# A chunked recurrence in which v is centred while it is transposed

## The chip, the cores and the metric

The kernel runs on one core of one Trainium2 chip. The metric is the time of one execution on the device, in microseconds, as the median of several runs. TensorE does matrix products, DVE (VectorE), ACT (ScalarE) and POOL (GpSimd) do elementwise work, SP (SyncE) issues most of the transfers. Each of them has a queue of its own that it works through in the program's order.

## The reference

One block of a hybrid model on 1024 tokens of width 1024: two normed and modulated inputs, a softmax attention with forget gates ("fox", 8 heads of 64) beside a recurrence ("rwkv7", 8 heads of 64), their gated sum, and a convolutional feed-forward layer. Cut to what matters here, the recurrence keeps a 64 x 64 state per head and ends in a normalisation over the 64 value channels of each head:

```python
def step(state, inp):
    r_t, w_t, k_t, v_t, a_t, b_t = inp
    sa = jnp.einsum('bhvk,bhk->bhv', state, a_t)
    state = state * w_t[:, :, None, :] + sa[..., None] * b_t[:, :, None, :] + v_t[..., None] * k_t[:, :, None, :]
    y_t = jnp.einsum('bhvk,bhk->bhv', state, r_t)
    return state, y_t
...
mean = jnp.mean(y, axis=-1, keepdims=True)
var = jnp.mean(jnp.square(y - mean), axis=-1, keepdims=True)
y = ((y - mean) * lax.rsqrt(var + GN_EPS)).reshape(bsz, seq, RWKV_WIDTH) * ln_w + ln_b
bonus = (jnp.sum(r_h * k_h * r_k, axis=-1, keepdims=True) * v_h).reshape(bsz, seq, RWKV_WIDTH)
return ((y + bonus) * g).astype(p.dtype)
```

Every row of the state belongs to one value channel, and the rows never mix: state and y are linear in v, channel by channel. So a v whose mean over the 64 channels of a head is taken away gives a y whose mean is zero. The bonus needs v as it is.

## The kernel before, in words

The program has stages one after the other: norms and input products, the recurrence, the attention, the branch products, and the feed-forward layer. Large products are split in a high and a low part (three products in fp32r for one in fp32).

**Units.** The recurrence works on 8 units, one for each pair of heads p = 0..3 and half of the sequence hf = 0, 1; a unit has 8 chunks of 64 tokens. Names end in p_hf: X1_0 is the tile X of pair 1, first half. `pre` (L759 to L867) prepares a unit: decays, norms, the products p1 of keys and receptances inside each chunk, masked into E (L823), then v and the a-vectors transposed into `vt` and `at` (L843, L844) and copied to UV (ACT, L849) and QA (DVE, L850), and q (L861). `inverse` (L732 to L757), called the solve here, inverts the 32 x 32 triangles: 31 steps of two small DVE instructions each (L740, L744). Its matrix goes through DRAM on the way in (sm, then M, L831 and L835) and on the way out (se, then TT, L747 and L754). `main` (L869 to L974) takes TT up: DVE transposes a piece of it into X (two instructions, L881, one for each head), TensorE makes xi, zi, uw and mz, then the state is carried through the 8 chunks (sp, yp, L930 to L944).

**The tail of a unit.** y is copied from PSUM (L951). `head_sums` sums it over the 64 channels of each head: a cast to fp32r on ACT, the remainder on POOL, and two products with the block matrix blk_r (mu). DVE subtracts the mean (L959), ACT squares (L961), a second `head_sums` gives the variance (va), and DVE and ACT finish.

**What sets the order.** TensorE's order is written out while the program is built, by a planner (`Weave`) with a clock of estimated costs. Chains (`main_chain` for the units one behind the other, `pre_chain`, and a spawned solve for each unit) say with `yield n` that their next piece is due n nanoseconds later; until then the planner lays in pieces of other stages, the "big products" of 128x128 by 128x512 (ps_rkv, qk, v, gt). `main` waits for the planner's `ready` time of the unit's solve (L836, L879), but only if that lies ahead when its turn comes. DVE, ACT, POOL and SP are ordered by the scheduler of the language from the program's dependencies. PSUM has 4 banks for `gen` tiles and 2 for big products; DVE's L365, L391, L336 or L992 frees a bank of the latter.

Of the kernel before, what the change touches and what calls it, by code (L numbers as in the profile page):

```python
# [9 lines left out]
F32 = mybir.dt.float32  # L10
F32R = mybir.dt.float32r
AF = mybir.ActivationFunctionType
ALU = mybir.AluOpType
# [5 lines left out]
NH = 512  # L19
# [3 lines left out]
CH = 64  # L23
# [112 lines left out]
def hybrid_block(ctx: ExitStack, tc: tile.TileContext, a, out):  # L136
    nc = tc.nc
# [3 lines left out]
    def mm(o, lhsT, rhs, start, stop, more=False):  # L141

        weave.mm_cost(o, lhsT, rhs)
        weave.last = nc.tensor.matmul(o, lhsT, rhs, start=start, stop=stop, skip_group_check=more)  # L144
# [4 lines left out]
    def transpose(o, i, eye):  # L149
        weave.now += 0.84 * max(math.prod(i.shape[1:]), i.shape[0])  # L150
        nc.tensor.transpose(o, i, eye)  # L151

    def f32(ap):
        return ap.bitcast(F32)

    tt, stt, ts = nc.vector.tensor_tensor, nc.vector.scalar_tensor_tensor, nc.vector.tensor_scalar
# [19 lines left out]
    def C(name):  # L176
        o, k = CST[name]
        return cst[:, o : o + k] if o < NC1 else cst2[:, o - NC1 : o - NC1 + k]

    eye_r, tri_r = C("ident"), C("tri")  # L180
    ident, ones = f32(eye_r), f32(C("ones"))
# [160 lines left out]
    with ExitStack() as es:  # L342
# [7 lines left out]
        def gen(name):  # L350
            return pr.tile([128, NH], F32, tag="gen", name=name)
# [358 lines left out]
        rw = es.enter_context(tc.tile_pool(name="rw", bufs=1, reuse_waits="tile"))  # L710
# [9 lines left out]

        blk_r = rw.tile([128, 128], F32R, name="blk_r")
        nc.scalar.copy(blk_r, C("blk"))

        def head_sums(ps, x, hi, lo):

            nc.scalar.copy(hi, x)
            nc.gpsimd.tensor_tensor(lo, x, f32(hi), op=ALU.subtract)
            yield 3400
            mm(ps, blk_r, hi, start=True, stop=False)
            mm(ps, blk_r, lo, start=False, stop=True)  # L730
# [28 lines left out]
        def pre(k, p, hf):  # L759

            n = f"{p}_{hf}"
            cs = slice(hf * NH, hf * NH + NH)
            rr, kk, vv = rkv[p, hf]
# [52 lines left out]
            for c0 in range(0, NCU, 4):  # L816
                ps = [gen(f"p1_{n}{h}{c0}") for h in range(2)]
                for c in range(c0, c0 + 4):
                    for h in range(2):
                        mm(ps[h][:, (c - c0) * 128 : (c - c0) * 128 + 128], bk[HS[h], c, BKS[h], :], ar[HS[h], :, c, :],  # L820
                           start=True, stop=True)
# [18 lines left out]
            vt, at = gen(f"vt{n}"), gen(f"at{n}")  # L840
            for b in range(4):
                bs = slice(b * 128, b * 128 + 128)
                transpose(vt[:, bs], vv[:, bs], ident)  # L843
                transpose(at[:, bs], ar[:, 0, 2 * b : 2 * b + 2, :], ident)  # L844
            v4 = vt.rearrange("p (b h s) -> p b h s", h=2, s=CH)
            a4 = at.rearrange("p (b h s) -> p b h s", h=2, s=CH)
# [22 lines left out]
        def main(k, p, hf):  # L869
            o = units.pop((p, hf))  # L870
            n = f"{p}_{hf}"
# [38 lines left out]
            Zt = rw.tile([128, NCU, CH], F32, tag="Zt", name=f"Zt{n}", bufs=1)  # L910
            Mt = rw.tile([128, NCU, CH], F32, tag="Mt", name=f"Mt{n}", bufs=1)
# [11 lines left out]
            yp = py.tile([128, NCU, CH], F32, tag="yp", name=f"yp{n}")  # L923
# [23 lines left out]
                S0 = state[p] = S1  # L947
            passed.add((k, 1))

            y = rw.tile([128, NH], F32, tag="y", name=f"y{n}", bufs=1)  # L950
            nc.scalar.copy(y, yp.rearrange("p c s -> p (c s)"))  # L951

            def part(nm, i):
                return rw.tile([128, NH], F32R, tag=nm, name=f"{nm}{i}{n}", bufs=1)

            mu = gen(f"mu{n}")
            yield 700
            yield from head_sums(mu, y, part("Zt", "r"), part("Mt", "r"))
            stt(y, mu, -1.0 / CH, y, op0=ALU.mult, op1=ALU.add)  # L959
            ysq = rw.tile([128, NH], F32, tag="ysq", name=f"ysq{n}", bufs=1)  # L960
            nc.scalar.activation(ysq, y, AF.Square)  # L961
            yield 2700
            va = gen(f"va{n}")
            yield from head_sums(va, ysq, part("Zt", "s"), part("Mt", "s"))
            rs = rw.tile([128, NH], F32, tag="ysq", name=f"rs{n}", bufs=1)
# [37 lines left out]
        def pre_chain():  # L1003
            for k, (p, hf) in enumerate(order):
                while got[p, hf] < 3:
                    weave.step()
                yield from pre(k, p, hf)
                if p < 3:
                    weave.first.extend(rkv_items(p + 1, hf))
                yield 0  # L1010

        def main_chain():
            for k, (p, hf) in enumerate(order):
                while (p, hf) not in units:
                    yield 200
                yield from main(k, p, hf)
                yield 0
# [877 lines left out]
    for s, k in enumerate(ORDER):  # L1895
# [22 lines left out]
        for tp in range(4):  # L1918
            r = ssq[:, 16 + tp : 17 + tp]
# [86 lines left out]
```

## Time and profile before

| what | value |
|---|---|
| median of 3 runs | 1670.34 us (1670.2 to 1674.31) |
| profiled execution | 1675.3 us, span 1673.2 us |
| mean granted clock of TensorE | 0.986 |
| TensorE busy | 1622.3 us, 97% |
| DVE busy | 1227.8 us, 73% |
| ACT busy | 808.3 us, 48% |
| POOL busy | 147.8 us, 9% |

Of the span, the recurrence takes roughly 165 to 620 us. In rows of groups the columns are line, engine, operation, tiles written and read, shape and count, then busy time in us and mean of one in ns, then the engine's idle time before them and what ended it. In rows of the timeline they are the start in us, the length in us, engine, line, operation, tiles and count, and in brackets the idle time before and its releaser; a row may stand for several instructions in a row. In rows of waits they are the waiting engine and instruction, what ended the wait, the total in us, the number and the longest. In rows of windows they are the stretch, its length, then busy time and instructions of TensorE's products, its weight loads, DVE, ACT and POOL, the granted clock, the share of the DMA engines and GB/s. Products in fp32 (not fp32r) stand in the trace as two records each.

### The profile page before, as it was taken

How to read it: one execution, taken by the hardware profiler on the slowest of the kernel's cores; microseconds unless marked ns; L12 is line 12 of the kernel's file. 1: busy time of each engine (PE TensorE's matmuls, PEld its weight loads, DVE VectorE, ACT ScalarE, POOL GpSimd, SP SyncE). 2: the span in 40 equal slices, each digit the busy share in tenths (PEclk: the TensorE clock that was granted, in tenths of full speed). 3: DMA queues.
4: the chain of work that ended last, by engine and by line, in shares of the span. 5: the costliest groups of instructions: out<-in, count | busy, mean ns of one | idle time of the engine just before them, and what ended most of it. 6: DMA issues, size and time to landing. Idle time of an engine off the chain costs nothing.

```text
span 1673.2 us, 26056 instructions
## 1 busy us (share of the span) xinstructions
PE 1622.3 (97%) x9772; PEld 1333.2 (80%) x9772; DVE 1227.8 (73%) x2390; ACT 808.3 (48%) x1482; POOL 147.8 (9%) x175
## 2 busy tenths in 40 slices
PE   5899999999999998999999999999999999999998
PEld 4677877787977777888878888888888888888886
DVE  5786787888876635888778445897777777786677
ACT  5453343434455545767623244654444444455455
POOL 0010101111111012322022000000000000000000
PEclk8899999999999999999999999999999999999999
DMA  8497744433343236433197420143223323574463
GB/s 333 133 327 213 194 124 130 129 102 113 96 127 92 80 112 155 127 113 119 36 344 264 164 89 39 63 131 108 102 95 99 116 95 108 190 274 154 129 210 107
DMA packets 120974, 239.85 MB, mean 143 GB/s; under 512 B 39888, under 2 KB 48336, under 8 KB 120848
## 3 DMA queue, kind: packets, MB, share of 16 engines
q1 hardware_dynamic: 112896, 220.94, 40.8%
q0 software_dynamic: 7952, 17.25, 3.9%
q8 instruction: 77, 1.26, 0.3%
q14 instruction: 49, 0.40, 0.1%
HBM read 172.59 MB, written 65.54 MB: 142 GB/s over the span
## 4 chain that ended last, share of the span: by engine, by line
PE 82%; DVE 9%; DMA 4%; ACT 3%; issue 2%; SPq 1%; POOL 0%; DVEq 0%; ACTq 0%
PE X L144 13%; PE D L144 13%; PE Y L144 6%; PE gt L144 6%; PE ps_rkv L144 6%; PE wo L144 5%; PE br L144 5%; PE rk_ps L144 4%; PE W L144 3%; PE v L144 2%; PE lg L144 2%; PE ov L144 2%; PE tp L151 2%; PE qk L144 2%; PE low L144 1%
## 5 line engine op out<-in xcount | busy, mean ns | idle before, releaser
L144 PE MATMUL D<-op,op 128*128 128x512 f32 x924 | 209.8, 389 | 0.0
L144 PEld LDWEIGHTS D<-op,op 128*128 128x128 f32 x924 | 173.3, 188 | 36.3 <-DVE op L1269 0.3
L144 PE MATMUL X<-T_m,S 128*128 128x512 f32 x440 | 107.2, 390 | 0.1
L144 PEld LDWEIGHTS X<-T_m,S 128*128 128x128 f32 x440 | 82.4, 188 | 18.2 <-ACT T_m L1694 0.5
L1268 ACT CAST op<-g 128x512 fp32r<-128x512 f32 x77 | 47.8, 621 | 73.8 <-PE D L144 47.9
L1269 DVE TENSOR_TENSOR op<-g,op 128x512 fp32r<-128x512 f32 x77 | 53.0, 688 | 41.5 <-ACT op L1268 41.5
L1505 DVE SCALAR_TENSOR_TENSOR c<-ab,vec,c 128x512 f32<-128x512 f32 x88 | 65.8, 749 | 19.5 <-ACT c L1508 17.9
L1469 DVE TENSOR_TENSOR S<-ur,S 128x512 fp32r<-128x512 f32 x66 | 45.5, 691 | 35.9 <-ACT S L1465 35.7
L270 DVE TENSOR_TENSOR lo_in<-raw_in,hi_in 128x512 fp32r<-128x512 f32 x84 | 57.9, 727 | 14.0 <-PE gt L144 5.0
L1465 ACT CAST S<-ur 128x512 fp32r<-128x512 f32 x66 | 41.0, 622 | 55.8 <-DVE ur L1458 30.9
L1469 DVE TENSOR_TENSOR A<-ur,A 128x512 fp32r<-128x512 f32 x64 | 44.0, 687 | 30.9 <-ACT A L1465 30.7
L268 ACT CAST hi_in<-raw_in 128x1024 fp32r<-128x1024 f32 x42 | 43.9, 1048 | 44.4 <-PE ps_rkv L144 26.6
L740 DVE TENSOR_TENSOR t<-E,M 128x60 f32<-128x60 f32 (+24 forms) x248 | 56.0, 226 | 12.0 <-DMA M<-sm 5.7
L144 PE MATMUL Y<-T_h,A 128*128 128x512 f32 x264 | 63.5, 389 | 0.0
L144 PE MATMUL Y<-T_h,S 128*128 128x512 f32 x264 | 63.3, 389 | 0.0
L744 DVE TENSOR_TENSOR E<-E,t 128x60 f32<-128x60 f32 (+24 forms) x248 | 56.8, 229 | 5.8
L144 PE MATMUL X<-B_b,A 128*128 128x512 f32 x252 | 60.8, 390 | 0.0
L144 PE MATMUL W<-B_f,A 128*128 128x512 f32 x252 | 60.6, 389 | 0.0
L1090 ACT ACTIVATE P<-lg,nm 128x896 f32<-128x896 f32 (+3 forms) x64 | 47.4, 743 | 22.8 <-DVE nm L1086 22.6
L144 PEld LDWEIGHTS Y<-T_h,A 128*128 128x128 f32 x264 | 49.5, 188 | 10.4
L144 PEld LDWEIGHTS Y<-T_h,S 128*128 128x128 f32 x264 | 49.5, 188 | 10.3
L1465 ACT CAST A<-ur 128x512 fp32r<-128x512 f32 x64 | 39.8, 623 | 34.1 <-PE X L144 29.4
(473 smaller groups left out, 4151.9 us busy)
## 6 DMA issues: line engine op xcount, KB each, us to landing
raw_in<-in_w_in SPq DMA_DIRECT2D x50, 512.0 KB, 4.3
wm<-in_w_mod SPq DMA_DIRECT2D x48, 512.0 KB, 7.4
ur<-in_w_up SPq DMA_DIRECT2D x44, 512.0 KB, 4.3
g<-d_g SPq DMA_DIRECT2D x35, 512.0 KB, 3.9
d_g<-gs SPq DMA_DIRECT2D x44, 256.0 KB, 2.0
d_g<-c SPq DMA_DIRECT2D x33, 256.0 KB, 4.6
d_st<-qh SPq DMA_DIRECT2D x64, 128.0 KB, 2.4
d_gate<-gs SPq DMA_DIRECT2D x32, 256.0 KB, 2.7
```

Of the source, the lines that this page charges most:

```text
L144: weave.last = nc.tensor.matmul(o, lhsT, rhs, start=start, stop=stop, skip_group_check=more)
L151: nc.tensor.transpose(o, i, eye)
L268: nc.scalar.copy(hi, raw)
L270: nc.vector.tensor_tensor(lo[:, c : c + NH], raw[:, c : c + NH], f32(hi[:, c : c + NH]), op=ALU.subtract)
L740: i = tt(tv, E32[:, 0:J, s : s + 1].to_broadcast([128, J, W]), M32[:, s : s + 1, s + 1 : 32].to_broadcast([128, J, W]), op=ALU.mult)
L744: tt(E32[:, 0:J, s + 1 : 32], E32[:, 0:J, s + 1 : 32], tv, op=ALU.add)
L1090: nc.scalar.activation(e[:, 0:n], lg[:, 0:n], AF.Exp, bias=nm[:, 0:1], accum_out=nm[:, 1:2])
L1268: nc.scalar.copy(hi, src)
L1269: tt(lo, src, f32(hi), op=ALU.subtract)
L1465: nc.scalar.copy(hi, src)
L1469: tt(lo, src, f32(hi), op=ALU.subtract)
L1505: stt(c, ab[:, x + hf * NH : x + hf * NH + NH], V("conv_w", 22 * x + i), c, op0=ALU.mult, op1=ALU.add)
```

## The change

The block matrix blk, whose fp32r copy is kept in blk_r, is overwritten by cen = ident - blk / 64. In `pre` the transposes of v become products with cen as the moving operand: (v transposed) times cen is v transposed with the mean over the channels of each head taken away. y then has no mean. The first `head_sums`, its PSUM tile and the subtraction go; the square reads PSUM directly, ahead of the copy of y. The bonus still takes v as it was. The waits in the tail go from 700 + 3400 + 2700 + 3400 to 1300 + 3400.

```diff
         blk_r = rw.tile([128, 128], F32R, name="blk_r")
         nc.scalar.copy(blk_r, C("blk"))
+        cen = C("blk")
+        stt(cen, cen, -1.0 / CH, ident, op0=ALU.mult, op1=ALU.add)
...
             for b in range(4):
                 bs = slice(b * 128, b * 128 + 128)
-                transpose(vt[:, bs], vv[:, bs], ident)
+                mm(vt[:, bs], vv[:, bs], cen, start=True, stop=True)
                 transpose(at[:, bs], ar[:, 0, 2 * b : 2 * b + 2, :], ident)
...
+            yf = yp.rearrange("p c s -> p (c s)")
+            ysq = rw.tile([128, NH], F32, tag="ysq", name=f"ysq{n}", bufs=1)
+            nc.scalar.activation(ysq, yf, AF.Square)
             y = rw.tile([128, NH], F32, tag="y", name=f"y{n}", bufs=1)
-            nc.scalar.copy(y, yp.rearrange("p c s -> p (c s)"))
+            nc.scalar.copy(y, yf)
...
-            mu = gen(f"mu{n}")
-            yield 700
-            yield from head_sums(mu, y, part("Zt", "r"), part("Mt", "r"))
-            stt(y, mu, -1.0 / CH, y, op0=ALU.mult, op1=ALU.add)
-            ysq = rw.tile([128, NH], F32, tag="ysq", name=f"ysq{n}", bufs=1)
-            nc.scalar.activation(ysq, y, AF.Square)
-            yield 2700
+            yield 1300
             va = gen(f"va{n}")
             yield from head_sums(va, ysq, part("Zt", "s"), part("Mt", "s"))
```

How the order moves is shown at three places. A row has the line, the instruction, the tile written, the tiles read, and its shape; in the changed kernel the lines from L723 on are higher by two up to the tail, so L740 and L744 of the solve read L742 and L746, L850 reads L852 and L881 reads L883. Units are in the tiles' names.

On DVE, from the last instruction of the solve of unit 1_0 to the transposes of X1_0, before:

```order
L744 TENSOR_TENSOR E321_0_2651<-E321_0_2651,t321_0_2653 128x8
L823 TENSOR_TENSOR E1_1_3046<-p1_1_100_3049,cst2_120 128x4x128
L823 TENSOR_TENSOR E1_1_3046<-p1_1_110_3050,cst2_120 128x4x128
L270 TENSOR_TENSOR lo_in22_3074<-raw_in22_3071,hi_in22_3073 128x512 x2
L365 SCALAR_TENSOR_TENSOR k20_2753<-ps_rkv60_2997,omu_80,sh_rkv60_3066 128x512
L359 MEMSET sh_rkv100_3379 128x1
L959 SCALAR_TENSOR_TENSOR y0_1_3043<-mu0_1_3045,y0_1_3043 128x512
L823 TENSOR_TENSOR E1_1_3046<-p1_1_104_3100,cst2_120 128x4x128
L823 TENSOR_TENSOR E1_1_3046<-p1_1_114_3101,cst2_120 128x4x128
L270 TENSOR_TENSOR lo_v00_3134<-raw_v00_3131,hi_v00_3133 128x512 x2
L881 STREAM_TRANSPOSE X1_0_3200<-TT1_0_2524 32x256 x2
```

and the same place in the changed kernel:

```order
L852 COPY QA1_1_3049<-at1_1_3130 64x4x64 x2
L742 TENSOR_TENSOR t321_0_2741<-E321_0_2739,M321_0_2582 128x24
L852 COPY QA1_1_3049<-at1_1_3130 64x4x64 x2
L746 TENSOR_TENSOR E321_0_2739<-E321_0_2739,t321_0_2741 128x8x3
L742 TENSOR_TENSOR t321_0_2741<-E321_0_2739,M321_0_2582 128x16
L746 TENSOR_TENSOR E321_0_2739<-E321_0_2739,t321_0_2741 128x8x2
L742 TENSOR_TENSOR t321_0_2741<-E321_0_2739,M321_0_2582 128x8
L746 TENSOR_TENSOR E321_0_2739<-E321_0_2739,t321_0_2741 128x8
L883 STREAM_TRANSPOSE X1_0_3047<-TT1_0_2587 32x256 x2
L270 TENSOR_TENSOR lo_v00_3182<-raw_v00_3179,hi_v00_3181 128x512 x2
L365 SCALAR_TENSOR_TENSOR r20_2819<-ps_rkv20_3099,omu_80,sh_rkv20_3174 128x512
```

Before, nine rows of other work stood between the solve's end and X; now none does, and the copies of at1_1 to QA1_1, which came behind X, stand inside the solve.

On TensorE, at the transposes of unit 1_1 ahead of xi1_0, before:

```order
L151 MATMUL at1_1_3161<-cst_73,ar1_1_2902 128x128
L151 MATMUL vt1_1_3160<-cst_73,v11_2040 128x128
L151 MATMUL at1_1_3161<-cst_73,ar1_1_2902 128x128
L144 MATMUL ps_rkv100_3146<-u_hi_110,hi_in22_3073 128x512 x6
L144 MATMUL ps_rkv100_3146<-u_lo_111,hi_in22_3073 128x512 x4
L144 MATMUL va0_1_3121<-Zts0_1_3122,blk_r_1174 128x512
L144 MATMUL va0_1_3121<-Mts0_1_3123,blk_r_1174 128x512
```

(16 transposes tb1_1, the 16 small products q1_1 and then xi1_0 follow), and in the changed kernel:

```order
L144 MATMUL vt1_1_3129<-cst2_120,v11_2041 128x128
L151 MATMUL at1_1_3130<-cst_73,ar1_1_2916 128x128
L144 MATMUL vt1_1_3129<-cst2_120,v11_2041 128x128
L151 MATMUL at1_1_3130<-cst_73,ar1_1_2916 128x128
L144 MATMUL ps_rkv20_3099<-u_hi_110,lo_in14_3016 128x512 x3
L144 MATMUL xi1_0_3150<-X1_0_3047,E1_0_2434 32x32 x16
L144 MATMUL ps_rkv20_3099<-u_hi_110,lo_in14_3016 128x512 x5
L144 MATMUL ps_rkv100_3194<-u_hi_110,hi_in22_3093 128x512 x7
L144 MATMUL zi1_0_3202<-TT1_0_2587,X1_0_3047 32x32 x16
```

Ten big products, va, tb and q stood between the last at1_1 and xi1_0; now three big products do, and tb and q come after zi1_0.

On DVE, from the end of the solve of unit 2_1 to X2_1, before:

```order
L744 TENSOR_TENSOR E322_1_4690<-E322_1_4690,t322_1_4692 128x8
L802 TENSOR_TENSOR al3_0_4846<-al3_0_4846,k30_4068 128x512
L941 TENSOR_SCALAR S2_06_5099<-sp2_0_4905,pcd2_0_3556 128x64
L803 TENSOR_TENSOR bk3_0_5001<-al3_0_4846,en3_0_4994 128x8x64
L807 SCALAR_TENSOR_TENSOR ksq3_0_5013<-r30_4067,vec_72,al3_0_4846 128x512
L941 TENSOR_SCALAR S2_07_5111<-sp2_0_4905,pcd2_0_3556 128x64
L336 SCALAR_TENSOR_TENSOR gs0_0_5128<-gt0_0_5078,gs0_0_5128 128x512
L959 SCALAR_TENSOR_TENSOR y2_0_5115<-mu2_0_5117,y2_0_5115 128x512
L823 TENSOR_TENSOR E3_0_5155<-p1_3_000_5158,cst2_120 128x4x128
L823 TENSOR_TENSOR E3_0_5155<-p1_3_010_5159,cst2_120 128x4x128
L270 TENSOR_TENSOR lo_in15_5195<-raw_in15_5192,hi_in15_5194 128x512 x2
L881 STREAM_TRANSPOSE X2_1_5235<-TT2_1_4544 32x256 x2
```

and in the changed kernel, where the masks of p1_3_000 and p1_3_010 stand eleven solve steps ahead of the solve's end:

```order
L746 TENSOR_TENSOR E322_1_4772<-E322_1_4772,t322_1_4774 128x8
L825 TENSOR_TENSOR E3_0_5127<-p1_3_004_5153,cst2_120 128x4x128
L825 TENSOR_TENSOR E3_0_5127<-p1_3_014_5154,cst2_120 128x4x128
L270 TENSOR_TENSOR lo_in15_5181<-raw_in15_5178,hi_in15_5180 128x512 x2
L336 SCALAR_TENSOR_TENSOR gs0_1_5171<-gt0_1_5119,gs0_1_5171 128x512
L883 STREAM_TRANSPOSE X2_1_5005<-TT2_1_4640 32x256
L852 COPY QA3_0_5128<-at3_0_5208 64x4x64 x4
L883 STREAM_TRANSPOSE X2_1_5005<-TT2_1_4640 32x256
```

The end of the solve has moved closer to X2_1, and the copies of at3_0 lie between its halves. The number of gate products that the planner lays ahead of the attention is the same in both (18 halves of 24).

## The prediction

> **What bounds the kernel now.** I read the page's busy times, then the busy times of the stretch from 165 to 640 us in which the recurrence runs, then who TensorE waited for in it.
>
> ```profile
> PE 1622.3 (97%) x9772; PEld 1333.2 (80%) x9772; DVE 1227.8 (73%) x2390; ACT 808.3 (48%) x1482; POOL 147.8 (9%) x175
> ```
>
> ```profile
> 165.00:640.00 475.00, 465.11 (x4322) 375.01 (x4321) 342.19 (x959) 215.67 (x377) 66.51 (x83) 1.00 0.45 121
> ```
>
> ```profile
> PE rk_ps L144 <- ACT gm L1191: 4.6, 1, 4.6
> PE qk L144 <- DVE v L365: 2.2, 1, 2.2
> PE sp L144 <- DVE S L941: 1.5, 3, 0.9
> PE zi L144 <- ACT X L888: 0.6, 1, 0.6
> PE q L144 <- DVE QA L850: 0.4, 1, 0.4
> ```
>
> TensorE works 465 of these 475 us, at the full granted clock (1.00), since large products of other stages are laid between the steps of the recurrence. What it waits for adds up to 9.3 us, 4.6 of it at the start of the attention. So two things count here: TensorE's own work, and any wait that stops its one queue. Work taken off DVE, ACT or POOL is worth nothing by itself.
>
> **The change, part by part.** *The two products for the mean* go, 16 in all:
>
> ```profile
> 615.53 0.40 PE L144 MATMUL mu<-Ztr,blk_r 128*128 128x512 f32 x1
> 615.77 0.39 PE L144 MATMUL mu<-Mtr,blk_r 128*128 128x512 f32 x1
> 615.99 0.39 PE L144 MATMUL gt<-u_hi,hi_in 128*128 128x512 f32 x1
> ```
>
> From the first to the next stranger's start is 0.46 us, so 8 units give 8 x 0.46 = 3.7 us of TensorE back. *The four transposes of v* per unit become fp32 products with the matrix `cen`. The nearest rows are those transposes, and the fp32 products 128x128x128 of another stage (64 in the program, x128 in the trace, so each is two records):
>
> ```profile
> 176.41 0.27 PE L151 MATMUL vt<-cst,v 128*128 128x128 f32 x1
> 176.52 0.27 PE L151 MATMUL at<-cst,ar 128*128 128x128 f32 x1
> L144 PE MATMUL tr<-dg,h_sb 128*128 128x128 f32 x128 | 14.8, 275 | 0.0
> ```
>
> A transpose takes 0.11 us from start to start, a product 2 x 14.8 / 128 = 0.23 us. 32 of them cost 32 x 0.12 = +3.8 us. TensorE's own work thus stays where it was: -3.7 + 3.8 = +0.1 us (from -4, if they ran as the transposes do, to +3.8, if the removed pair had cost nothing; neither end is likely, with rows this near).
>
> The Trainium skill's page "TensorE: Matmul & The Clock Gate" (Terms) says that transpose mode is four times faster for FP32, and "Perfetto Trace Analysis" (Optimizing Tensor Performance) that a logical transpose should not be a standard matmul. By that the 32 products would cost 32 x 3 x 0.11 = +10.6 us and the sum below would end 6.8 us higher; the tr row of this trace says twice, not four times.
>
> *Off TensorE* go eight each of the DVE subtraction, the cast (like that of ysq) and POOL's low half:
>
> ```profile
> L959 DVE SCALAR_TENSOR_TENSOR y<-mu,y x8: 680/691/692, 269.2 to 616.8; 128x512 f32<-128x512 f32 x8
> L726 ACT CAST Zts<-ysq x8: 618/621/625, 270.6 to 618.2; 128x512 fp32r<-128x512 f32 x8
> L727 POOL TENSOR_TENSOR Mtr<-y,Ztr x8: 1284/1299/1320, 265.1 to 612.6; 128x512 fp32r<-128x512 f32 x8
> ```
>
> They take 0.69, 0.62 and 1.30 us. The ACT square now reads PSUM ahead of the copy of y, and one DVE instruction makes `cen` early on. None is on TensorE's path by the waits above, so I price them at nothing; if all of DVE's 8 x 0.69 = 5.5 us were on the path after all, that would be the gain of a rival below.
>
> *The yields* are the part that moves things. Ahead of the variance's products the planner now puts 1300 + 3400 in place of 700 + 3400 + 2700 + 3400, 5.5 us less per unit. The chains of the units run one behind the other, so the next unit's `xi` comes sooner, and it needs the solve (`inverse`), whose 62 small DVE instructions and two DRAM round trips stand where they stood. How tight this is, before:
>
> ```profile
> 568.49 0.18 DVE L744 TENSOR_TENSOR E<-E,t 128x8 f32<-128x8 f32 x1
> 568.73 2.52 SPq L747 DMA_DIRECT2D se<-E  x4
> 572.90 1.83 SPq L754 DMA_DIRECT2D TT<-se  x4
> 576.71 0.90 DVE L881 STREAM_TRANSPOSE X<-TT 32x256 f32<-32x256 f32 x2 [4.12 <-DMA TT<-se]
> 577.64 0.75 DVE L968 SCALAR_TENSOR_TENSOR y<-y,vec,rs 128x512 f32<-128x512 f32 x1
> 577.85 0.69 PE L144 MATMUL xi<-X,E 32*32 32x32 f32 x32
> ```
>
> That is the last unit. From the solve's last instruction (ended at 568.67) to the X transposes are 8.0 us of DMA there and back; DVE stands idle for 4.1 of them with y behind it, and xi starts 0.24 us after X. In the first unit the same trip took 219.91 to 226.13, and the second half 0.27 us more:
>
> ```profile
> 219.74 0.17 DVE L744 TENSOR_TENSOR E<-E,t 128x8 f32<-128x8 f32 x1
> 226.13 0.43 DVE L881 STREAM_TRANSPOSE X<-TT 32x256 f32<-32x256 f32 x1 [3.82 <-DMA TT<-se]
> ```
>
> I take 7.5 us, between 6.2 and 8.0. (In the changed order two loads of M for the next solve are issued on SP between se and TT of unit 1_0; SP waits there for se to land anyway, 571.25 to 572.90, so they cost nothing.) In unit 1_0 nothing waited before:
>
> ```profile
> 310.64 0.17 DVE L740 TENSOR_TENSOR t<-E,M 128x8 f32<-128x8 f32 x1
> 310.85 0.17 DVE L744 TENSOR_TENSOR E<-E,t 128x8 f32<-128x8 f32 x1
> 321.65 0.27 PE L151 MATMUL at<-cst,ar 128*128 128x128 f32 x1
> 321.90 0.89 DVE L881 STREAM_TRANSPOSE X<-TT 32x256 f32<-32x256 f32 x2
> 323.50 1.72 DVE L850 COPY QA<-at 64x256 f32<-64x256 f32 x4
> 326.44 0.69 PE L144 MATMUL xi<-X,E 32*32 32x32 f32 x32
> ```
>
> There the solve ended 10.9 us ahead of X, and the copies of `at` came behind X. In the changed order (the rows quoted with the change) the copies of `at1_1` stand between the last steps of the solve of 1_0, X stands right behind its last instruction, and on TensorE only three big products lie between the last `at1_1` transpose and `xi1_0`. DVE takes its queue in order, so the wait can be counted from that transpose on, whatever went on before:
> - four copies, 1.72 us, and six solve steps at 0.21 us (310.64 to 310.85), 1.3 us: 3.0
> - the trip, 7.5
> - X, 0.89, and 0.24 to xi: 1.1
>
> That is 11.6 us, less the three products that TensorE has meanwhile (0.23 each, by 615.77 to 615.99), 0.7: **TensorE stops for about 10.9 us at xi1_0** (9.6 with the trip at 6.2, 11.4 with 8.0; more where DVE runs late).
>
> In unit 2_1 (third place) X stood nine rows of DVE work behind the solve's end and now stands four behind it, and the `at3_0` copies lie between its two halves. From the end of the first `p1_3_0..` products on TensorE, DVE has 0.39 us to start, two masks, eleven solve steps, the trip, X, four copies, X:
>
> ```profile
> 318.37 1.29 DVE L823 TENSOR_TENSOR E<-p,cst 128x512 f32<-128x512 f32 x2 [0.39 <-PE p L144]
> 317.17 1.16 PE L144 MATMUL p<-ar,bk 64*128 64x128 f32 x16
> ```
>
> 0.39 + 1.29 + 11 x 0.21 + 7.5 + 0.43 + 1.72 + 0.43 + 0.24 = 14.3 us. TensorE has 28 big products (6.4), the second half of p (1.2 by the row) and the four vt and at (4 x 0.34 = 1.4), 9.0 us. Wait: 5.3 us.
>
> In unit 2_0 the DVE stretch from the `v` of the pair behind (L365, reading ps_rkv101) to the solve's end is 21 solve steps (4.4), two states (0.6), a scan (1.2), two splits (1.3) and four operations of 128x512 (2.9), 10.4 us; with ACT's shifted copy ahead (0.7), the trip, X with one y step between its halves (1.6) and 0.24 that is 20.4. TensorE has 62 big products (14.3), four steps of the state (4 x 0.38, from 309.43 to 309.81) and two pairs of sums (0.9), 16.7. Wait: 3.7 us, between nothing and 4.5.
>
> ```profile
> 309.43 0.33 PE L144 MATMUL sp<-S,Mt 64*64 64x64 f32 x4
> 309.81 1.65 PE L144 MATMUL ps_rkv<-u_hi,lo_in 128*128 128x512 f32 x6
> L362 ACT ACTIVATE sh_rkv<-ps_rkv,vec 128x512 f32<-128x512 f32 x24 | 16.6, 690 | 17.9 <-PE ps_rkv L144 16.5 <-issue 1.2
> L941 DVE TENSOR_SCALAR S<-sp,pcd 128x64 f32<-128x64 f32 x8 | 2.2, 279 | 2.2 <-PE sp L144 2.1
> L781 DVE TENSOR_TENSOR_SCAN cum<-cst,cum 128x512 f32<-128x512 f32 x1 | 1.2, 1217 | 0.0
> L803 DVE TENSOR_TENSOR bk<-al,en 128x512 f32<-128x512 f32 x1 | 0.7, 689 | 0.0
> ```
>
> The other five units keep their place: counted the same way, DVE's work and the trip end some 0.5 to 2.5 us ahead of xi, so DVE stands still there and TensorE does not. Behind X in unit 1_0 wait the split of w_v and the L365 that frees a bank; TensorE has 12 big products in hand there (2.8 us), which cover them.
>
> **The sum.** The products +0.1, unit 1_0 +10.9, 2_1 +5.3, 2_0 +3.7: +20.0 us. Against it, some of the 4.7 us of small waits before 620 us should fall away while the others catch up; I take 1.5. So +18.5 us, on the profiled execution's 1675.3 us about 1694. That execution is 5 us above the median of the runs (1670.34), so **1689 us** for the median. The stretch's own wait (4.6 us at rk_ps) stands behind it all and stays.
>
> **Rivals.**
> *No change, 1670 us.* The planner's order is tight on paper only: if the trip were short and DVE ahead, TensorE would wait for nothing, and the products cancel. For it: they do cancel, and the order has as many big products before the attention as it had. Against it: X cannot come before its own trip, whose shortest case here is 6.2 us, and 0.7 us of TensorE's work lies against it. Chance 0.10.
> *Faster, 1664 us.* DVE is busy 342 of 475 us, and the waits on it (2.2 + 1.5 + 0.4) with the 0.6 are 4.7 us. Were the freed 5.5 us of DVE to remove them all, and the products to cost as transposes (-3.7 in all), the time falls by up to 8 us, likely 6. It decides only if the moved X waits are absent. Against it: the 2.2 us stand at 228 us, in unit 0_0, where the order is as before. Chance 0.07.
>
> ```profile
> 228.11 1.21 PE L144 MATMUL qk<-u_hi,hi_in 128*128 128x512 f32 x4 [2.23 <-DVE v L365]
> ```
>
> *Only the one wait, 1680 us.* 2_0 and 2_1 are differences of large sums; if DVE is ahead there, 10.9 - 1.5 + 0.1 are left. Chance 0.20.
> *More, 1697 us.* The products at four times a transpose (+6.8), or DVE late into unit 1_0 and a bank not freed behind X (2.2 us in the first unit). Chance 0.10.
> The forecast, 1689, holds the remaining 0.53; its own range is 1683 to 1694.
>
> **The numbers.** A measurement of this kernel tells 0.3%, 5.0 us, from no change. Slower is the forecast, the one wait and more: 0.83; same 0.10; faster 0.07. The range from 1673 to 1697 leaves out the two cases that are not slower and a little above.
>
> **What would show it.** The waits of the changed kernel should have xi behind X (or X behind the DMA TT) as TensorE's largest, 9 to 12 us near 320 us, with DVE idle some 7 us just ahead of X there; a second of 3 to 7 near 475; `vt` as x64 records, 0.11 us each; TensorE's busy time in the page unchanged within 1 us. Wrong it is if xi follows the three ps_rkv products without a gap, or if the vt products take 0.4 us each.

## The result, and the profile after

| | before | after |
|---|---|---|
| median of 4 runs | 1672.32 us (1670.2 to 1674.43) | 1698.29 us (1696.5 to 1705.57) |
| profiled execution | 1675.3 us, span 1673.2 us | 1705.57 us, span 1703.8 us |
| mean granted clock of TensorE | 0.986 | 0.975 |

The changed kernel takes 1.0165 times as long, with a 95% interval of 1.0135 to 1.0196: 26 us by the medians, 30.3 us by the two profiled executions (that of the changed kernel is the slowest of its four). The forecast had the direction and the place, and was too small: 1689 us, in a range that ended at 1697.

Where the time lies is told first by the start of the attention, the first `lg` product. In the timeline of the kernel before it is

```profile
644.67 0.39 PE L144 MATMUL lg<-stA 128*128 128x512 f32 x1
```

and in that of the changed kernel

```profile
675.30 0.39 PE L144 MATMUL lg<-stA 128*128 128x512 f32 x1
```

30.6 us later. From there to the end of the span it is 1028.5 us in both. All that was lost, was lost ahead of that product. The windows from the start to the first `lg`, of the kernel before and of the changed one, split it (the second and third numbers are the length and TensorE's busy time):

```profile
0.00:644.67 644.67, 609.43 (x4916) 486.00 (x4916) 456.68 (x1130) 298.82 (x505) 79.94 (x105) 0.97 0.53 155
0.00:675.30 675.30, 619.80 (x4931) 496.42 (x4932) 450.98 (x1123) 292.14 (x497) 68.40 (x97) 0.95 0.50 149
```

TensorE is idle 55.5 instead of 35.2 us, 20.3 more, and busy 10.4 us longer. The waits of TensorE between 150 and 680 us of the changed kernel (what waits, what ended it, total in us, number, longest):

```profile
PE xi L144 <- DVE X L883: 18.4, 6, 10.8
PE rk_ps L144 <- ACT gm L1190: 4.8, 2, 4.6
PE qk L144 <- DVE v L365: 3.8, 1, 3.8
PE v L144 <- DVE lo_v L270: 2.3, 1, 2.3
```

Before, xi didn't wait at all. TensorE's timeline at the unit 1_0:

```profile
322.37 0.38 PE L144 MATMUL vt<-cst,v 128*128 128x128 f32 x2
322.59 0.27 PE L151 MATMUL at<-cst,ar 128*128 128x128 f32 x1
322.70 0.39 PE L144 MATMUL vt<-cst,v 128*128 128x128 f32 x2
...
323.62 0.95 PE L144 MATMUL ps_rkv<-u_hi,lo_in 128*128 128x512 f32 x3
335.38 0.28 PE L144 MATMUL xi<-X,E 32*32 32x32 f32 x2 [10.82 <-DVE X L883]
336.23 1.06 PE L144 MATMUL xi<-X,E 32*32 32x32 f32 x30 [0.56 <-DVE X L883]
337.21 2.50 PE L144 MATMUL ps_rkv<-u_hi,lo_in 128*128 128x512 f32 x5
```

DVE at the same place (the solve's last instruction, then X):

```profile
328.46 0.17 DVE L746 TENSOR_TENSOR E<-E,t 128x8 f32<-128x8 f32 x1
334.81 0.43 DVE L883 STREAM_TRANSPOSE X<-TT 32x256 f32<-32x256 f32 x1 [6.17 <-DMA TT<-se]
335.73 0.44 DVE L883 STREAM_TRANSPOSE X<-TT 32x256 f32<-32x256 f32 x1 [0.50 <-DMA TT<-se]
```

and SP with the trip through DRAM between them:

```profile
328.87 2.56 SPq L749 DMA_DIRECT2D se<-E  x4
...
332.85 1.80 SPq L756 DMA_DIRECT2D TT<-se  x4
```

This is the picture that was forecast: after `vt`, `at` and three big products TensorE has nothing it may do, and DVE stands idle for 6.2 us behind the trip. A `vt` product takes 0.22 us from its start to that of the next instruction, an `at` transpose 0.11.

What wasn't forecast stands in the last row: five big products from 337.21 to 339.51, 0.46 us each, where a big product took 0.23 us. The windows of the kernel before and of the changed one (the last three numbers are the granted clock, the DMA share and GB/s):

```profile
330.00:440.00 110.00, 109.15 (x1201) 93.88 (x1201) 89.35 (x266) 45.56 (x85) 16.57 (x22) 1.00 0.39 110
440.00:530.00 90.00, 89.89 (x845) 72.39 (x842) 70.92 (x203) 45.12 (x78) 12.59 (x16) 1.00 0.35 100
```

```profile
330.00:440.00 110.00, 100.23 (x1011) 84.00 (x1011) 76.35 (x229) 39.23 (x71) 11.31 (x20) 0.91 0.32 89
440.00:530.00 90.00, 84.33 (x937) 73.55 (x938) 62.74 (x181) 35.91 (x69) 8.98 (x13) 0.94 0.38 107
```

Before, the clock was granted whole. Now it is 0.91 and 0.94: it is halved for stretches behind the stops. By the trace's record of the granted clock there is one such stretch of 13.7 us from 329.2 us, one of 6.8 from 359.9, 3.4 from 441.9 and 6.8 from 506.7, and one of 6.8 from 230.2, where before there was none between 59.7 and 636.6 us. The stops that go with the last four, in TensorE's timeline:

```profile
230.90 1.22 PE L144 MATMUL qk<-u_hi,hi_in 128*128 128x512 f32 x2 [3.77 <-DVE v L365]
...
360.07 1.40 PE L144 MATMUL v<-lo_v,u_hi 128*128 128x256 f32 x4 [2.27 <-DVE lo_v L270]
...
440.23 0.22 PE L144 MATMUL xi<-X,E 32*32 32x32 f32 x2 [1.72 <-DVE X L883]
441.24 0.69 PE L144 MATMUL xi<-X,E 32*32 32x32 f32 x30 [0.79 <-DVE X L883]
...
506.39 0.22 PE L144 MATMUL xi<-X,E 32*32 32x32 f32 x2 [2.77 <-DVE X L883]
508.39 1.05 PE L144 MATMUL xi<-X,E 32*32 32x32 f32 x30 [1.78 <-DVE X L883]
```

Counted by their starts, 11, 12, 8 and 9 big products run at 0.43 instead of 0.23 us behind the stops at 230, 335, 440 and 506 us: 40 x 0.2 = 8.0 us. Behind that at 360 us stand none of 128x512, but 21 of 128x256, at 0.23 instead of 0.12 us (eight take 1.87 us from 362.02 on, three took 0.36 from 356.80): 2.3 us. That is 10.3 us of the 10.4.

### The profile page after: what moved, and what is told of

It is laid out like the page before. It is cut to its first block, busy times and chain, and to the rows that moved or that the text cites. A ratio compares the mean times of both kernels' runs of the same rounds, so it can differ in the third digit from the quotient of the medians.

```text
span 1703.8 us, 26049 instructions
## 1 busy us (share of the span) xinstructions
PE 1632.5 (96%) x9788; PEld 1343.6 (79%) x9788; DVE 1223.2 (72%) x2383; ACT 802.1 (47%) x1474; POOL 135.7 (8%) x167
## 4 chain that ended last, share of the span: by engine, by line
PE 82%; DVE 9%; DMA 4%; ACT 2%; issue 2%; SPq 1%; DVEq 0%; ACTq 0%
PE X L144 13%; PE D L144 12%; PE Y L144 6%; PE gt L144 6%; PE wo L144 5%; PE br L144 5%; PE ps_rkv L144 5%; PE rk_ps L144 4%; PE W L144 3%; PE qk L144 3%; PE v L144 3%; PE lg L144 2%; PE ov L144 2%; PE tp L151 2%; PE low L144 1%
## 5 line engine op out<-in xcount | busy, mean ns | idle before, releaser
L742 DVE TENSOR_TENSOR t<-E,M 128x60 f32<-128x60 f32 (+24 forms) x248 | 57.1, 230 | 10.9 <-DMA M<-sm 5.1
L746 DVE TENSOR_TENSOR E<-E,t 128x60 f32<-128x60 f32 (+24 forms) x248 | 55.6, 224 | 5.8
L144 PEld LDWEIGHTS Y<-T_h,A 128*128 128x128 f32 x264 | 49.5, 188 | 10.4
L144 PEld LDWEIGHTS Y<-T_h,S 128*128 128x128 f32 x264 | 49.6, 188 | 10.3
```

The costliest lines, as they stand in the source:

```text
L742: i = tt(tv, E32[:, 0:J, s : s + 1].to_broadcast([128, J, W]), M32[:, s : s + 1, s + 1 : 32].to_broadcast([128, J, W]), op=ALU.mult)
L746: tt(E32[:, 0:J, s + 1 : 32], E32[:, 0:J, s + 1 : 32], tv, op=ALU.add)
```

## The experiments

The theory after the result: the new order alone makes the loss; it consists of TensorE's stops at xi and of a halved clock behind each stop; the products with `cen` and the square that reads PSUM cost what was forecast. The rivals: the products cost more (four times a transpose), or the square and the copy now both reading PSUM hold something up; or one tight unit makes all of it. In the expectations the theory is Theory 1 and the dearer products or PSUM reads are Rival A; Theory 3 is that a stop costs its own length and no more.

**The old waits in the tail.** The changed kernel, with the time between the copy of y and the variance as it was, 700 + 3400 + 2700 = 6800:

```diff
-            yield 1300
+            yield 6800
```

> The changed kernel with the tail's wait of 1300 set to 6800, so that the order of the large products and the place of every X is as before (the distance from p1 to xi is within 1.5 us of the kernel before's in all units but 2_0, where it is longer). Theory 1 (the loss is the stops of TensorE at xi, and the halved clock that follows each): no wait at xi over 1 us, one halved stretch at most near 230 us, time 1668 to 1674. Rival A (the products with cen, or the square from PSUM, cost the time): no gain from the order, 1690 or more.

Measured: 1672.7 us (9 runs, 1666.43 to 1676.75), 0.9988 of before, interval 0.9971 to 1.0005. The waits in the same stretch:

```profile
PE qk L144 <- DVE v L365: 3.3, 1, 3.3
PE sp L144 <- DVE S L943: 2.4, 4, 0.8
PE rk_ps L144 <- ACT gm L1190: 1.4, 2, 1.2
```

No xi waits, the stop at rk_ps is 1.2 instead of 4.6 us, and that at qk stays (3.3 us, with a halved stretch of 3.4 us and 7 slow products behind it). One number was put back, all 32 products and the PSUM reads stayed, and the loss is gone. The order makes it; what the products and the PSUM reads add lies within the interval, some 3 us to either side.

**Transposes in place of the products**, in the order of the run before (the planner was told the products' cost). This kernel leaves the centring out:

```diff
-                mm(vt[:, bs], vv[:, bs], cen, start=True, stop=True)
+                transpose(vt[:, bs], vv[:, bs], ident)
+                weave.now += 160.32 - 107.52
```

> As the run with the old yields, but v is transposed again instead of multiplied with cen, so the mean of y is left out of the computation altogether; TensorE's order is row by row the same. This prices the 32 products by themselves. By the rows of the trace (0.23 against 0.11 us) it is 3.8 us below that run; if a product cost four transposes, 10.6 us below; if the products were hidden, equal.

Measured: 1667.83 us (6 runs, 1664.67 to 1671.48), 0.9956 of before (0.9941 to 0.997), 4.9 us below the run with the products. The forecast's row gave 3.8 us, the rule of four times 10.6. The intervals of the two ratios (each some 2.5 us to either side) don't tell 3.8 from 4.9; they leave 10.6 out. With the starts in the trace (0.22 and 0.11 us) a product costs about twice a transpose here.

**The solves called ready later.** If the planner knew that X comes later, it would put TensorE's work there, and the stops at xi would go:

```diff
-            ready = weave.now + (47500 if k == 0 else 38500)
+            ready = weave.now + (52000 if k == 0 else 47000)
```

> The changed kernel with the planner's ready time of a solve set to 47000 instead of 38500 ns after its load (52000 instead of 47500 for the first unit); the short tail stays. The distance from p1 to xi becomes 53 to 74 us. Theory 1: the waits at xi vanish, in the first unit too (3.8 us and its halved clock), so 1663 to 1671, at or below the kernel before. Rival A: no change from the changed kernel, 1690 or more. Theory 3 (a stop costs only its own length): also at about 1670, since the waits go.

Measured: 1695.95 us (4 runs, 1692.31 to 1699.57), 1.0119 of before (1.01 to 1.0139). A miss by some 25 us; the time is one that Rival A had named, but its cause is excluded by the first run. The waits, and the first `lg`:

```profile
PE sp L144 <- DVE S L943: 5.7, 4, 3.2
PE v L144 <- DVE vs L991: 3.5, 1, 3.5
PE lg L144 <- DMA stB<-d_st: 2.9, 1, 2.9
PE xi L144 <- DVE E L746: 2.6, 1, 2.6
```

```profile
665.27 0.39 PE L144 MATMUL lg<-stA 128*128 128x512 f32 x1
```

The xi waits went as meant, from 18.4 to 2.8 us. The chain of the units stayed long: the first `lg` is 20.6 us behind that of before, with 48 more big products (a gate, about 11 us) laid ahead of it. That work is missing in the attention: from the first `lg` to the end of the span (1697.8 us) are 1032.5 us, 4.0 more than in the changed kernel, although 11 us of products had been taken from there. The windows from the first `lg` to the end, of this run and of the changed kernel:

```profile
665.27:1697.80 1032.53, 1011.06 (x4810) 844.87 (x4808) 771.00 (x1258) 505.00 (x967) 66.35 (x70) 0.98 0.40 136
675.30:1703.80 1028.50, 1012.75 (x4858) 847.16 (x4856) 772.22 (x1260) 509.95 (x977) 67.28 (x71) 0.99 0.41 136
```

TensorE is idle 5.7 us longer there and busy only 1.7 us less, not 11. By the record of the clock it ran at half for 34.0 us of this stretch instead of 14.7, which is up to 9.6 us of slower products. So with fewer products to lay between, the stops moved on (to sp and v, and to lg and others in the attention), and there too they were paid with their length and with a halved clock.

**One unit called ready later**, that of the longest stop alone:

```diff
-            ready = weave.now + (47500 if k == 0 else 38500)
+            ready = weave.now + (47500 if k == 0 else 48500 if k == 2 else 38500)
```

> The changed kernel with the ready time of unit 1_0 alone later by 10000 ns: its distance from p1 to xi goes from 46.7 to 56.5 us, those of 2_0 and 3_0 fall by 2 to 3 us. Theory 1: the 11.4 us wait at xi1_0 falls to 2 us or less, with it the halved clock near 337 us (12 slow products, 2.4 us) and the 2.3 us wait of v_0 behind X with its own halved stretch: 12 to 16 us off, 1682 to 1687. Theory 3 (a stop costs only its own length): 9 to 10 us off, 1688 to 1690. Rival A: nothing off.

Measured: 1697.53 us (4 runs, 1696.56 to 1698.01), 1.0135 of before (1.012 to 1.0151): another miss, at the time of Rival A, whose cause the first run excludes. The wait row of xi, and the two units in the timeline:

```profile
PE xi L144 <- DVE X L883: 17.6, 6, 9.5
```

```profile
333.39 0.22 PE L144 MATMUL xi<-X,E 32*32 32x32 f32 x2 [2.04 <-DVE X L883]
...
433.65 0.28 PE L144 MATMUL xi<-X,E 32*32 32x32 f32 x2 [9.55 <-DVE X L883]
```

The stop of 10.8 us at xi1_0 shrank to 2.0; that of xi2_0 grew from 1.7 to 9.5. The sum of the xi waits is 17.6 instead of 18.4 us. So it isn't a single tight place: the stop goes to another unit when it is closed here. The starts of xi from unit to unit, in us, show the same:

| | from unit to unit | first to last |
|---|---|---|
| before | 49, 48, 47, 58, 47, 52, 47 | 349 |
| old waits in the tail | 49, 48, 47, 59, 47, 52, 47 | 350 |
| changed | 44, 60, 51, 54, 66, 50, 59 | 383 |
| one unit ready later | 43, 61, 43, 57, 69, 46, 59 | 378 |

Laid 5.5 us closer by the planner, the units come at 44 us once, and then at 60; the mean goes from 50 to 55 us.

**What a stop costs.** Onto the kernel with the old waits, one stop of chosen length was put in the fifth unit: 1, 4 or 18 copies of 128x256 on POOL, and a small product `dm` that needs the last of them. These copies and the product add work; their result isn't used.

```diff
+            if k == 4:
+                da = rw.tile([128, 256], F32, tag="X", name="da", bufs=1)
+                for _ in range(1):
+                    nc.gpsimd.tensor_copy(da, y[:, 0:256])
+                dm = gen("dm")
+                nc.tensor.matmul(dm[:, 0:256], ident, da, start=True, stop=True)
```

> The kernel with the old yields (no wait at xi), and one stop of TensorE put in by hand in unit 2_0, where it was never idle: behind the last yp it must wait for one POOL copy of a 128x256 piece of y, and then makes one small product that nobody reads. The stop is ACT's copy and the POOL copy, some 1.5 to 2 us. Theory 1 (a stop over about 2 us is followed by some us at half the granted clock, a shorter one mostly not): clock 1.0 throughout there, the stretch longer by the stop alone. Theory 3 (a stop costs its own length): the same.

> The same with four POOL copies: a stop of some 3 to 3.5 us. Theory 1: a stretch of 3.4 or 6.8 us at clock 0.5 begins at its end, with 7 to 14 big products at 0.43 instead of 0.23 us, 1.4 to 2.8 us on top of the stop. Theory 3: none of that.

> The same with eighteen POOL copies: a stop of some 9 us. Theory 1: the clock is at 0.5 during the stop, and for up to 6.8 us behind it; on top of the stop 1.4 to 2.8 us, no more than behind the middle one, since it is the time to come back that costs, not the length. Theory 3: none.

Measured, one execution each: 1673.32, 1684.61 and 1690.8 us, beside 1672.38 for the kernel before. In the timelines, the stop, the eight big products after it and the first `lg`; with one copy:

```profile
467.30 0.70 PE L962 MATMUL dm<-da,cst 128*128 128x256 f32 x2 [1.64 <-POOL da L960]
467.65 2.18 PE L144 MATMUL gt<-u_hi,lo_in 128*128 128x512 f32 x8
...
641.60 0.39 PE L144 MATMUL lg<-stA 128*128 128x512 f32 x1
```

with 4 copies:

```profile
476.50 1.22 PE L962 MATMUL dm<-da,cst 128*128 128x256 f32 x2 [7.36 <-POOL da L960]
477.16 3.98 PE L144 MATMUL gt<-u_hi,lo_in 128*128 128x512 f32 x8
...
653.58 0.39 PE L144 MATMUL lg<-stA 128*128 128x512 f32 x1
```

with 18 copies:

```profile
479.86 1.22 PE L962 MATMUL dm<-da,cst 128*128 128x256 f32 x2 [13.56 <-POOL da L960]
480.51 3.97 PE L144 MATMUL gt<-u_hi,lo_in 128*128 128x512 f32 x8
...
656.88 0.39 PE L144 MATMUL lg<-stA 128*128 128x512 f32 x1
```

The stops were meant to be 1.5 to 2, 3 to 3.5 and some 9 us. The two longer ones came out longer, since POOL took up other work between its first copy and the rest (4.4 us of it and of waiting, from 470.7 to 475.1 us, with four copies).

The eight products take 2.18 us behind the stop of 1.6 us, and 3.98 and 3.97 behind those of 7.4 and 13.6. From the beginning of the stop (start of `dm` less its idle time) to `lg` are 175.9, 184.4 and 190.6 us. Against the shortest that is 8.5 and 14.6 us more, for stops 5.7 and 11.9 us longer: the two longer stops cost 2.8 and 2.7 us on top of their length. In both, 11 big products and `dm` ran slow: from the start of `dm` to that of the next small product (p) it is 5.84 us, with one copy 3.14, 2.7 us less. So the addition is the same for a stop of 7 as for one of 14 us, and the stop of 1.6 us has none. The rest of the differences between the three times lies elsewhere, 3.5 us ahead of the stop with 4 copies and 1.9 us behind `lg` with 18.

**X laid behind the v of the first unit.** The stop at qk in the first unit stands because X is ahead of L365 in DVE's queue and waits for the trip there. With X due 300 ns ahead of `ready` instead of 1500, and xi 300 ns behind it (old waits in the tail):

```diff
-            yield max(0, o["ready"] - weave.now - 1500)
+            lead = 1500 if k else 300
+            yield max(0, o["ready"] - weave.now - lead)
...
-            yield 1500
+            yield lead
```

> The kernel with the old yields, and in unit 0_0 alone X is issued 300 instead of 1500 ns ahead of xi: on DVE X0_0 then stands behind the w_in split and the L365 that frees the bank, TensorE's order and the other seven units stay. Theory 1: the 3.3 us wait of qk at 227 us and its halved stretch (7 slow products, 1.4 us) go, xi0_0 waits at most 1 us: 3 to 5 us below the run with the old yields, 1667 to 1670, and 5 to 8 us below the kernel before. If DVE's head of queue was not the cause of that wait, it stays, and the time too.

Measured: 1671.39 us (12 runs, 1668.39 to 1674.06), 0.9988 of before (0.9978 to 0.9998), as without the edit. The timeline of TensorE tells why:

```profile
227.89 1.43 PE L144 MATMUL xi<-X,E 32*32 32x32 f32 x32 [2.32 <-DVE X L884]
229.25 3.78 PE L144 MATMUL qk<-u_hi,hi_in 128*128 128x512 f32 x8
```

qk no longer waits, but xi now does, 2.3 us. This stop is shorter than the one it replaced (3.3), and 12 slow products stand behind it instead of 7.

**And xi as far behind X as it was.** Same as the last, with the second wait left at 1500:

```diff
-            yield max(0, o["ready"] - weave.now - 1500)
+            yield max(0, o["ready"] - weave.now - (1500 if k else 300))
```

> The change with the old waits in the tail (6800 in place of 1300), and for the first unit alone the X transposes placed 300 ns instead of 1500 ns ahead of the due time of the solve, with xi 1500 ns behind them as it was. If a short stop is paid twice (its length, and a stretch of halved clock behind it), then taking away both the stop of 3.3 us at qk near 227 us, which X causes by standing ahead of L365 in DVE's queue, and the xi stop that takes its place when xi isn't moved too, gives the 3.3 us and the 1.4 us of slow products back: 1667 to 1669 us, with no stop over 1.5 us between 165 and 620 us and no halved clock there. If stops merely move on, as they did when one unit was made to wait, it stays at 1671 to 1673 with some other stop of 2 us or more in the first unit.

Measured: 1668.93 us (10 runs, 1665.81 to 1671.25), 0.9964 of before (0.9952 to 0.9976). The largest waits in the stretch, and the window that holds the first unit:

```profile
PE sp L144 <- DVE S L943: 2.2, 4, 0.8
PE sp L144 <- DVE sh_rkv L361: 1.4, 1, 1.4
PE rk_ps L144 <- ACT gm L1190: 1.4, 2, 1.2
```

```profile
220.00:330.00 110.00, 105.41 (x1020) 81.91 (x1020) 83.76 (x240) 43.48 (x77) 12.62 (x20) 1.00 0.49 130
```

No stop over 1.4 us, the clock whole from 54 to 705 us, and the time that was expected. This version computes all of the change and is faster than both kernels, by 5.6 us (before, in the same set of runs) and by some 29 (changed, by the medians of two sets).

## Why the prediction was right and wrong

**The products, +0.1 us: right.** `vt` takes 0.22 us and a transpose 0.11; with the old order the whole change stands at 0.9988 of before.

**The three stops: right in place and nearly in size.** Forecast 10.9, 5.3 and 3.7 us, measured 10.82 + 0.56 = 11.4 (1_0), 2.77 + 1.78 = 4.6 (2_1) and 1.72 + 0.79 = 2.5 (2_0); 18.4 for 19.9. The cause is as put there: X stands right behind the solve's end, and its trip through DRAM (6.2 us of idle DVE; X begins 6.2 us after the solve's last instruction ended) has 0.7 us of TensorE's work against it. That 1_0 came out so near was partly luck: the trip took 6.2 us instead of 7.5, but the solve ended 4.8 us behind the last `at` transpose instead of 3.0, since other steps still stood ahead on DVE, and X's second half waited another 0.5.

**The small waits, -1.5 us: right.** Those on S, X to zi, and QA went from 1.5 + 0.6 + 0.4 to 0.6 us, -1.9.

**"Twelve big products cover what is queued behind X": right at that place, and short-sighted.** Nothing waited in the ten us after xi1_0. But TensorE's v waited 2.3 us at 360 us for a split that DVE reached late, after solve steps without a gap. And the wait at qk in unit 0_0, which I had left at 2.2 us since its order was as before, was 3.8. Together +3.9 us that the sum lacks.

**The step that failed: the sum itself, in which a stop costs its own length.** The clock of 1.00 was carried over to the changed kernel, and what runs slow behind a stop was put at nothing without a word. Each of the five stops above was followed by a halved clock, in all 10.3 us by the slow products counted. With it the account closes: products 0.1, xi 18.4, v 2.3, qk 1.6, p 0.7 (it didn't wait before), small waits -1.9, clock 10.3, together 31.5 for the 30.6 us by which `lg` is late. Agreement within a microsecond is better than the count deserves: small products ran slow in the same stretches too (30 xi in 1.06 us at 336.23, where 32 took 0.69 before), and other groups came out shorter by as much. The waits alone, forecast at +18.4, measured +20.3; 1689 + 10.3 would have been 1699. The 10.3 us are those of the profiled execution, whose clock was 0.975; the three others were granted 0.978 and 0.979 and took 5.6 to 9.1 us less.

The trace of before had shown this price. Behind its one long stop, at the attention's start, eight big products took 3.78 us where eight take about 2:

```profile
637.38 3.78 PE L144 MATMUL rk_ps<-u_hi,hi_in 128*128 128x512 f32 x8 [4.64 <-ACT gm L1191]
```

I quoted the 4.6 us as a wait, and took the clock of 1.00 in the stretch up to 640 us as given. Ahead of that stop the longest wait there was one of 2.23 us, and no halved clock followed it.

**What would show it: the busy time was wrong.** xi behind X, DVE idle ahead of it and the 64 `vt` records came; the second xi stop was within 3 to 7 us, though at 506 us instead of near 475. TensorE's busy time was to stay within 1 us, and the page of the changed kernel has:

```profile
PE 1632.5 (96%) x9788; PEld 1343.6 (79%) x9788; DVE 1223.2 (72%) x2383; ACT 802.1 (47%) x1474; POOL 135.7 (8%) x167
```

It rose by 10.2 us for 16 more records. That is the halved clock again: a slow product counts as busy for longer.

**The rivals.** "No change" and "faster" needed the trip to be covered, and it wasn't. "Only the one wait" (1680) fell: 2_0 and 2_1 waited too. "More" (1697) was next to the measured time, but by products at four times a transpose, which the run with transposes excludes, and by a late bank behind X in 1_0, where nothing waited; the bank's wait in 0_0 (qk) grew by 1.6 us, and the stop of 2.3 us at 360 was for a split.

**After the result** I erred twice in one way: I took the stops as places that can be mended one by one. Called ready later, one unit passed its stop on to another, and all units together passed it on to the attention. What the runs showed as the remedy is the 5.5 us in each unit's tail that the change had taken out.

Of the clock, the Trainium skill says in "TensorE: Matmul & The Clock Gate" (Part 1: The HAM clock gate) that it is either whole or half, that it is judged in windows of about 3.4 us which run on their own, and that it falls to half after at least one idle window. The halved stretches here, 3.4, 6.8 and 13.7 us, agree with such windows. The idle time doesn't: stops of 2.27 us (at 360 us) and 2.32 us (the run with X behind v), shorter than one such window, were enough, while 2.23 us (before, at 228 us) and 1.64 us weren't. The page also puts the ramp at under 1% of a typical span; 10.3 of 1704 us agrees, and is still a third of what this change cost.

## What to carry to other kernels

A stop of an engine that is otherwise full is priced at its length plus what runs slow behind it: here about 0.2 us for each of 7 to 12 big products, 1.4 to 2.7 us a stop, for all stops above 2.3 us and for some that were a little shorter. Waits written into a hand-made order may be the only room in which a slower chain (here two trips through DRAM and 62 small instructions for each unit) keeps up; whoever removes the work between them should leave the time, and then look which stop is next. A closed stop is only a gain when the summed waits fall, not when its own row does.

## What the runs showed of the hardware that was not expected

The price behind a stop did not grow with it where two lengths were tried: 2.7 us behind 7.4 us and behind 13.6 us. It also doesn't shrink evenly: a stop of 2.3 us was followed by 12 slow products, one of 3.3 us by 7, one of 2.23 us by none.

Which it is goes by when the stop falls, as the traces' records of the granted clock show. In all eleven traces the clock changes only at points that lie a multiple of 3.41 us apart, and each execution meets these points at another place. They cut the time into windows. Between 150 us and the first `lg`, 22 windows at full clock had TensorE idle for 1.85 us or more, and the next window ran at half in every case. All others had 1.64 us of idle time or less, and only one of them was followed by half the clock (1.63 us, in the run with all solves called ready later). The stop of 2.23 us before lies across two windows, 1.16 us in one and 1.06 in the other; of that of 2.32 us, 2.13 lie in one. The time at half clock behind a stop also ends at such a point: the two long stops of the experiment ended 6.0 and 5.9 us ahead of it, so their equal price is in part chance.

The stop at rk_ps ended when ACT was done, which had waited 5.6 us for the transfer of the last gate to DRAM (d_gate<-gs), before and in the changed kernel. With the old waits in the tail ACT met its wait for such a transfer one gate earlier (3.2 us at 627.77 us), and rk_ps stood for 1.2 us. Why the transfer lay otherwise there stays open.
